# Low parts of weight chunks by ScalarE and an accumulating DMA, selection steps at another rate, and value products one portion later

## The chip, the core and the metric

The kernel runs on one core of a Trainium2 chip. The core has a matrix engine (PE, with weight loads shown apart as PEld), three engines for elementwise work (DVE is VectorE, ACT is ScalarE, POOL is GpSimd), an engine that issues DMAs (SP), and 16 DMA engines that all queues share. The metric is the device time of one execution in microseconds (us). One execution of the kernel was profiled; its trace gives every instruction with its start, its duration and what released it.

## What is computed

Two layers of a transformer block over 528 tokens (16 meta tokens ahead of 512) with 1024 channels. Per layer, cut to what matters here:

```python
proj = einsum('btd,de->bte', rms_norm(x), w_in)       # 1024 x 4808 weights
q, k, v, gate_a, u_b, gate_b, q_idx, k_idx, w_idx, merge = split(proj)
q = rope(rms_norm(q)); k = rope(rms_norm(k)); q_idx = rope(q_idx); k_idx = rope(k_idx)
score = sum_h relu(q_idx . k_idx) * w_idx             # 8 index heads
sel   = top_k(score, 128)                             # of the visible keys, per query
attn  = softmax(q . k over sel) @ v                   # 8 heads of 64
y_a   = (attn * silu(gate_a)) @ w_a
y_b   = (pool(u_b) * silu(gate_b)) @ w_b
out   = x + (sig(merge_a) * y_a + sig(merge_b) * y_b) @ w_out
```

Nothing is rounded to fewer bits on the way to the output: a product of float32 matrices is made of three products of a faster format (F32R), high x high, high x low and low x high, where the high part is the value rounded to that format and the low part is what is left.

## The kernel before, in words

**Weights.** They come in 54 chunks of 2048 columns per partition, 27 per layer, used in a fixed order: one for keys and values, two for index queries, two for gate_b, two for u_b, one for half of the queries, two for gate_a, one for the other queries, two for w_b, then eight for the merge gates (`mixed` chunks, prepared otherwise), two for w_a and four for w_out. A chunk is two raw halves of 128 x 1024 float32. `w_load` (L128) issues their DMAs on SP; there are three raw buffers, so a half is loaded when an older half is no longer read. For each half, preparation makes a high tile and a low tile of 128 x 1024 F32R, out of eight such tiles (tag `w`): `high` (L174) is a copy by ACT, `low` (L178) is a subtraction, raw minus high, by DVE. The items wait in `prep_q`; while a chunk is in use, the next one is prepared, and each finished group of matmuls takes one item (`group_done`, L295). What is left when the chunk is needed is done at once (`flush_prep`).

**Order.** PE and DVE do their instructions in the order in which the program writes them. ACT, POOL and the DMA queues are ordered by a planner at build time, which may move an instruction ahead of others that were written earlier.

**The selection.** Top-128 is 16 rounds over the score tiles of 128 queries: find the eight largest (MAX8), then overwrite them (MATCH_REPLACE8). Query tiles are taken in pairs, first the tiles 0 and 1, then the tiles 2 and 3 (with 400 and 528 keys); a half-round is one `yield` of `topk_steps` (L604), that is, MAX8 or MATCH_REPLACE8 for both tiles of the pair. The steps wait in `sel` and are slipped in between other DVE work by an account in `group_done`: every call on PE or DVE adds a price from `pe_cost` or `dve_cost` to a meter, and

```python
spare[0] += FULL * (pe.us - seen[0]) - (dve.us - seen[1])
spare[0] = min(spare[0], CAP)                  # CAP = 1.5
while spare[0] > 0 and sel:                    # one half-round, its price taken off
```

A DVE call over n elements per partition has the price 0.15 + 0.00104 n us. ACT, POOL and DMA calls have none. Whatever is left of the selection when its result is needed is done at once: `ensure(2)` (L1094), called by `logits` (L629) for the first head pair of the query tile 2, runs all the half-rounds left of tiles 2 and 3, one after the other.

**Attention.** A generator (L626 to L735) whose portions are pumped between the matmul groups of other work (w_b, then the merge gates). For head pair u of 16 there are three portions: `logits(u+1)`, `scale(u)` and `values(u-1)`; then `soft(u+1)` (DVE adds the selection mask, ACT takes the exponential) and `gated`; then `turn(u)` (PE transposes the probabilities, ACT copies them out of PSUM as `pt`, L684). `values` multiplies `pt` by V on PE (tag `v`).

**Query groups.** `q_post` (L532) handles each group of the two query chunks: two DVE products, ACT squares, DVE sums them, `inv_rms` (L409) adds a small constant (L411) and takes the power -0.5 (L412), both on POOL, and DVE multiplies by the result.

Of the kernel before, what the change touches and what calls it, by code (L numbers as in the profile page):

```python
# [10 lines left out]
AF = mybir.ActivationFunctionType  # L11
OP = mybir.AluOpType
# [9 lines left out]
EPS = 1e-6  # L22
# [5 lines left out]
NCOL = 968  # L28
LB = 6
R_ATT = (1.8, 1.7)  # L30
FULL = 0.88
CAP = 1.5
W0 = 3
LAG0 = 2
# [53 lines left out]
def tile_block(ctx: ExitStack, tc: tile.TileContext, x, meta, w_in, pool_w, w_a, w_b, w_out, rows, hgain, c_tab, out):  # L88
    nc = tc.nc
    act, gp = nc.scalar, nc.gpsimd  # L90
    pe, dve = Metered(nc.tensor, pe_cost), Metered(nc.vector, dve_cost)
# [16 lines left out]
    def w_rows(w, c0, cols):  # L108
        return w.rearrange("(k p) e -> p k e", p=128)[:, :, c0:c0 + cols]

    chunks = []
    mixed = set()
    for l in range(2):
        wi = w_rows(w_in[l], 0, w_in.shape[2])
        chunks.append([(wi[:, :, 512:640], 0), (wi[:, :, 2688:2816], 128)])
        mb = [3784, 4040, 4296, 4552]
        order = [2176, 2432, 1664, 1920, 1408, 1152, 0, 640, 896, 256]
        chunks += [[(wi[:, :, c:c + 256], 0)] for c in order]
        chunks += [[(w_rows(w_b[l], c, 512), 0)] for c in (0, 512)]
        mixed |= set(range(len(chunks), len(chunks) + 8))  # L120
        chunks += [[(wi[:, :, c:c + 256], 0)] for c in (*mb, 2760, 3016, 3272, 3528)]
        chunks += [[(w_rows(w_a[l], c, 512), 0)] for c in (0, 512)]
        chunks += [[(w_rows(w_out[l], c, 256), 0)] for c in (0, 256, 512, 768)]

    W = {"load": 0, "prep": 0, "use": 0}
    raws, ready = {}, {}

    def w_load():  # L128
        c = W["load"]
        if c >= len(chunks):  # L130
            return
        W["load"] += 1
        kt = chunks[c][0][0].shape[1]
        cols = 2048 // kt
        raws[c] = []
        for s in range(2):
            r = wpool.tile([128, kt // 2, cols], F32, tag="raw", name="raw", bufs=3)
            for src, o in chunks[c]:
                nc.sync.dma_start(r[:, :, o:o + src.shape[2]], src[:, s * kt // 2:(s + 1) * kt // 2, :])
            raws[c].append(r)  # L140

    prep_q = deque()
# [8 lines left out]
    def w_tile():  # L151
        return wpool.tile([128, 1024], F32R, tag="w", name="w", bufs=8)

    def w_prep_enqueue(eng=dve):
        c = W["prep"]
        if c >= len(chunks):
            return
        W["prep"] += 1
        kt = chunks[c][0][0].shape[1]
        cols = 2048 // kt  # L160
        ready[c] = {}
        if c in mixed:
            prep_q.extend(mixed_prep(c))
            return
        parts = ready[c] = ([], [])

        def split(which):
            t = w_tile().rearrange("p (k e) -> p k e", e=cols)
            parts[which].extend(t[:, k] for k in range(kt // 2))
            return t  # L170

        his = {}

        def high(s):  # L174
            his[s] = split(0)
            act.copy(his[s], raws[c][s])  # L176

        def low(s):  # L178
            eng.tensor_sub(split(1), raws[c][s], f(his[s]))
            if s == 1:  # L180
                del raws[c]
                w_load()

        def second():
            low(0)
            high(1)

        prep_q.extend((lambda: high(0), second, lambda: low(1)))

    def mixed_prep(c):  # L190

# [103 lines left out]
    def group_done():  # L295
# [9 lines left out]
        half_done()  # L305
        spare[0] += FULL * (pe.us - seen[0]) - (dve.us - seen[1])
        spare[0] = min(spare[0], CAP)
# [58 lines left out]
    mhalf = one.tile([128, 1], F32, name="mhalf")  # L366
# [39 lines left out]
            gp.tensor_tensor(tab, ctab, bc(g), op=OP.mult)  # L406
            gp.tensor_tensor(w.rearrange("p t (a d) -> p t a d", a=2), s4, sw(g), op=OP.mult)

    def inv_rms(o, i):  # L409
        if i is not None:  # L410
            gp.tensor_scalar(o, i, EPS, None, op0=OP.add)  # L411
        gp.tensor_tensor(o, o, mhalf[:o.shape[0], :1].to_broadcast(list(o.shape)), op=OP.pow)  # L412

    hhi = one.tile([128, KT, T], F32R, name="hhi")
    hlo = one.tile([128, KT, T], F32R, name="hlo")
# [116 lines left out]
    def q_post(t, ps, normed, dst):  # L532
        s, m = TOK[t]
        p3 = ps[:m, :256].rearrange("p (h d) -> p h d", h=4)
        t1 = tmp.tile([128, HB], F32, tag="tt", name="t1", bufs=6)
        t2 = tmp.tile([128, HB], F32, tag="tt", name="t2", bufs=6)
        v1 = t1[:m, :256].rearrange("p (h d) -> p h d", h=4)
        C, S = (Cq[:m, t], Sq[:m, t]) if normed else (ctab[:m, t], stab[:m, t])
        dve.tensor_tensor(v1, p3, C[:, None, :].to_broadcast([m, 4, 64]), op=OP.mult)
        dve.tensor_tensor(t2[:m, :256].rearrange("p (h a d) -> p h a d", h=4, a=2), swapped(ps[:m, :256], 4),  # L540
                          S.rearrange("p (a d) -> p a d", a=2)[:, None, :, :].to_broadcast([m, 4, 2, 32]), op=OP.mult)
        if normed:
            sq = tmp.tile([128, HB], F32, tag="tt", name="sq", bufs=6)
            act.activation(sq[:m, :256], ps[:m, :256], AF.Square, scale=HD ** -0.5)  # L544
            ss = small(4, "ss4")
            dve.tensor_reduce(ss[:m], sq[:m, :256].rearrange("p (h d) -> p h d", h=4), axis=AX.X, op=OP.add)
            rq = small(4, "rq")
            inv_rms(rq[:m], ss[:m])
        gp.tensor_tensor(t1[:m, :256], t1[:m, :256], t2[:m, :256], op=OP.add)  # L549
        if normed:  # L550
            qs = tmp.tile([128, 544], F32R, tag="L", name="qs", bufs=LB)[:, :512].rearrange("p (h c) -> p h c", h=4)
        else:
            qs = tmp.tile([128, 4, 128], F32R, tag="P", name="qs", bufs=3)

        def second():
            if normed:
                dve.tensor_tensor(v1, v1, rq[:m, :, None].to_broadcast([m, 4, 64]), op=OP.mult)
            act.copy(qs[:m, :, 0:64], v1)

        def third():  # L560
            dve.tensor_sub(qs[:m, :, 64:128], v1, f(qs[:m, :, 0:64]))

        def trans():
            tp = bank("a", F32R)
            for h in range(4):
                pe.transpose(tp[:, h * 128:h * 128 + m], qs[:m, h, :], identr[:m, :m])
            act.copy(dst, f(tp).rearrange("p (h c) -> p h c", h=4)[:, :, :m])
        later(second, 1)
        later(third, QN if normed else QI)
        later(trans, QN + 1 if normed else QI + 1)  # L570
# [55 lines left out]
    def attention(ensure):  # L626
# [17 lines left out]
        def soft(u):  # L644
            i, j = divmod(u, 4)
            n = NK[i]
            mn, sm = small(2, "mn"), small(2, "sm")
            L = {}
            for hh, pi, o, w, ps in st[u]:
                if pi == 0:  # L650
                    L[hh] = tmp.tile([128, 544], F32, tag="L", name="lt", bufs=LB)
                e = min(w, n - o)
                dve.tensor_tensor_reduce(L[hh][:, o:o + e], ps[:, :e], SC[i][:, n - 1::-1] if i == 0 else SC[i][:, o:o + e], 1.0,
                                         3e38 if pi == 0 else mn[:, hh:hh + 1], op0=OP.add, op1=OP.min,
                                         accum_out=mn[:, hh:hh + 1])
            for hh in range(2):
                act.activation(L[hh][:, :n], L[hh][:, :n], AF.Exp, scale=-1.0, bias=mn[:, hh:hh + 1],  # L657
                               accum_out=sm[:, hh:hh + 1])
            st[u] = L, sm

        def scale(u):
            i, j = divmod(u, 4)
            n = NK[i]
            L, sm = st[u]
            rs = small(2, "rs")
            dve.reciprocal(rs, sm)
            for hh in range(2):
                act.activation(L[hh][:, 16:n], L[hh][:, 16:n], AF.Copy, scale=rs[:, hh:hh + 1])  # L668
                dve.tensor_scalar(pms[i][:, 2 * j + hh, :], L[hh][:, 0:16], rs[:, hh:hh + 1], None, op0=OP.mult)
            st[u] = L  # L670
# [45 lines left out]
        for u in range(-1, 17):  # L716
            if u + 1 < 16:
                logits(u + 1)
            if 0 <= u < 16:
                scale(u)  # L720
            if u >= 1:
                values(u - 1)
                if u % 4 == 0:
                    meta_values(u // 4 - 1)
            yield
            if u + 1 < 16:
                soft(u + 1)
            if u >= 1 and u % 4 == 0:
                gated(u // 4 - 1)
            yield  # L730
            if 0 <= u < 16:
                turn(u)
                if u % 4 == 3:
                    meta_turn(u // 4)
            yield  # L735
# [217 lines left out]
    for l in range(2):  # L953
# [98 lines left out]
        for c in (1, 0):  # L1052
            w = chunk()
            for mi in (1, 0):
                j = 2 * c + mi
                u = tmp.tile([128, 544], F32, tag="L", name="u", bufs=LB)
# [158 lines left out]
        else:  # L1215
            for c in range(4):
                w = chunk()
                for t in range(1, 5):
                    s, m = TOK[t]
                    hf = 0 if t <= 2 else 1  # L1220
                    o = s - hf * HB
# [66 lines left out]
```

## Time and profile before

| | |
|---|---|
| median of 3 runs | 850.3 us (850.09, 850.3, 850.82) |
| the profiled execution | 851.3 us |
| its span, first to last instruction | 849.5 us |
| mean granted TensorE clock | 0.96 of full speed |
| instructions | 15773 |

The profiled execution is 1.8 us longer than its span: that lies ahead of the first and behind the last instruction. It is 1.0 us above the median. A row of the groups gives the operation, its tiles (written <- read), the count, the busy time in all and the mean of one in ns, then the idle time before it and what ended that. A row of the waits gives who waited for whom, the sum in us, how often, and the longest. In the table of stretches, each engine has its busy time and, in brackets, its instructions; PEclk is the granted clock.

### The profile page before, as it was taken

Reading aid. Unit: us, or ns where it says so; the run is one execution under the profiler, and the core shown is the slowest. Engines: PE = TensorE matmul, PEld = TensorE weight load, DVE = VectorE, ACT = ScalarE, POOL = GpSimd, SP = SyncE. Lnnn points to the kernel's source line nnn. Section 1 sums busy time; section 2 is a strip of 40 time slices with the busy share of each in tenths; the row PEclk is TensorE's granted clock in tenths of the full one; section 3 lists DMA queues with packets and bytes.
Section 4 is the critical chain, followed back from the end, with each engine's and each line's share of the span. In section 5 each row is a group of like instructions: output and inputs, shape, how many; then the busy total and the mean of one; then the engine's idle time right before and its main releaser. Section 6 shows DMA issues by size and latency. Waiting matters only on the chain.

```text
span 849.5 us, 15773 instructions
## 1 busy us (share of the span) xinstructions
PE 768.4 (90%) x5989; PEld 727.4 (86%) x5989; DVE 623.9 (73%) x1452; ACT 438.7 (52%) x1016; POOL 242.5 (29%) x266
## 2 busy tenths in 40 slices
PE   7999999987980999999999999999889269999998
PEld 5999999987870888999999989989768269999998
DVE  6776887759889776576447768878799987766622
ACT  5556534236760778643344565252568148874421
POOL 6540165063310121124345301642532011212400
PEclk9999999988995899999999999999999769999999
DMA  8422222211120121252513222221203003117231
GB/s 268 154 77 73 76 75 64 100 51 51 50 75 0 51 75 51 77 200 91 185 54 99 77 73 77 74 78 72 75 26 100 25 25 101 50 51 226 96 110 44
DMA packets 64171, 71.71 MB, mean 84 GB/s; under 512 B 2736, under 2 KB 55248, under 8 KB 64096
## 3 DMA queue, kind: packets, MB, share of 16 engines
q1 hardware_dynamic: 64096, 70.71, 26.5%
q8 instruction: 47, 0.77, 0.4%
q14 instruction: 28, 0.23, 0.1%
HBM read 64.28 MB, written 6.42 MB: 83 GB/s over the span
## 4 chain that ended last, share of the span: by engine, by line
PE 70%; DVE 21%; ACT 4%; POOL 3%; issue 2%; DMA 0%; SPq 0%; ACTq 0%; DVEq 0%; POOLq 0%
PE d L60 57%; PE a L60 10%; DVE sc L60 4%; PE v L60 4%; DVE m L60 3%; DVE w L60 3%; DVE t L60 3%; DVE x L60 1%; DVE hlo L60 1%; POOL rq L412 1%; DVE hsum L60 1%; POOL rq L411 1%; DVE raw L60 1%; DVE pm L60 1%; ACT lt L657 1%
## 5 line engine op out<-in xcount | busy, mean ns | idle before, releaser
L60 PE MATMUL d<-hhi,w 128*128 128x256 f32 (+3 forms) x1408 | 291.3, 298 | 0.0
L60 PEld LDWEIGHTS d<-hhi,w 128*128 128x128 f32 x1408 | 227.9, 190 | 7.3 <-issue 1.4
L60 DVE TENSOR_TENSOR w<-raw,w 128x512 fp32r<-128x512 f32 (+1 forms) x186 | 177.9, 966 | 23.9 <-ACT w L200 14.0
L60 PE MATMUL d<-hlo,w 128*128 128x256 f32 (+3 forms) x704 | 194.4, 295 | 0.6 <-POOL hlo L1155 0.6
L60 PE MATMUL d<-w,hhi 128*128 128x256 f32 (+2 forms) x928 | 145.6, 286 | 3.7 <-ACT w L176 2.7
L60 PEld LDWEIGHTS d<-hlo,w 128*128 128x128 f32 x704 | 133.5, 190 | 3.3 <-POOL hlo L1155 0.8
L60 PEld LDWEIGHTS d<-w,hhi 128*128 128x128 f32 (+1 forms) x928 | 125.7, 186 | 7.8 <-ACT w L176 3.1
L206 POOL TENSOR_TENSOR raw<-raw 128x512 f32<-128x512 f32 x32 | 41.6, 1302 | 237.3 <-DVE w L60 157.2
L176 ACT CAST w<-raw 128x1024 fp32r<-128x1024 f32 x76 | 79.5, 1049 | 16.8 <-PE d L60 13.9
L200 ACT CAST w<-raw 128x512 fp32r<-128x512 f32 x112 | 67.7, 619 | 34.9 <-POOL raw L206 16.4
L60 PE MATMUL d<-w,hlo 128*128 128x256 f32 (+2 forms) x464 | 85.4, 282 | 0.0
L60 PE MATMUL d<-hsum,w 128*128 128x264 f32 (+1 forms) x576 | 77.4, 289 | 0.0
L60 PEld LDWEIGHTS d<-hsum,w 128*128 128x128 f32 x576 | 72.3, 191 | 1.6 <-issue 1.2
L60 PE MATMUL a<-consts,lt 128*128 128x128 f32 x161 | 25.2, 284 | 51.2 <-ACT lt L668 48.3
L60 PEld LDWEIGHTS d<-w,hlo 128*128 128x128 f32 (+1 forms) x464 | 68.1, 187 | 0.4
L60 PEld LDWEIGHTS a<-consts,lt 128*128 128x128 f32 x161 | 18.9, 143 | 54.0 <-ACT lt L668 50.3
L668 ACT ACTIVATE lt<-lt,rs 128x128 f32<-128x128 f32 (+3 forms) x64 | 32.8, 559 | 53.6 <-DVE rs L60 53.5
L549 POOL TENSOR_TENSOR t<-t,t 128x256 f32<-128x256 f32 (+1 forms) x34 | 32.2, 947 | 95.5 <-DVE t L60 89.2
L60 PE MATMUL d<-mhi,w 128*128 128x272 f32 (+2 forms) x192 | 54.3, 363 | 3.2 <-ACT sq L544 2.9
L60 DVE MATCH_REPLACE8 sc<-m,sc 128x400 f32<-128x400 f32 (+2 forms) x100 | 54.3, 547 | 0.0
L60 DVE MAX8 m<-sc 128x8 f32<-128x400 f32 (+2 forms) x100 | 52.5, 554 | 0.6
L1155 POOL TENSOR_TENSOR hlo<-ta,hhi 128x256 fp32r<-128x256 f32 (+1 forms) x32 | 31.2, 988 | 57.5 <-PE d L60 42.5
(189 smaller groups left out, 1323.5 us busy)
## 6 DMA issues: line engine op xcount, KB each, us to landing
raw<-in_w_in_dram SPq DMA_DIRECT2D x72, 512.0 KB, 3.5
raw<-in_w_out_dram SPq DMA_DIRECT2D x16, 512.0 KB, 3.4
kept<-res SPq DMA_DIRECT2D x16, 264.0 KB, 2.7
res<-kept SPq DMA_DIRECT2D x16, 264.0 KB, 4.9
raw<-in_w_branch_b_dram SPq DMA_DIRECT2D x8, 512.0 KB, 3.6
raw<-in_w_branch_a_dram SPq DMA_DIRECT2D x8, 512.0 KB, 4.4
xt<-in_x_dram SPq DMA_DIRECT2D x4, 512.0 KB, 5.3
raw<-in_w_in_dram SPq DMA_DIRECT2D x8, 256.0 KB, 4.8
```

The source lines that it names most:

```text
L60: return fn(*a, **k)
L176: act.copy(his[s], raws[c][s])
L200: act.copy(t[:, 0], blk[src[n]])
L206: eng.tensor_tensor(blk[src[n]], blk[src[x]], blk[src[y]], op=op)
L411: gp.tensor_scalar(o, i, EPS, None, op0=OP.add)
L412: gp.tensor_tensor(o, o, mhalf[:o.shape[0], :1].to_broadcast(list(o.shape)), op=OP.pow)
L549: gp.tensor_tensor(t1[:m, :256], t1[:m, :256], t2[:m, :256], op=OP.add)
L657: act.activation(L[hh][:, :n], L[hh][:, :n], AF.Exp, scale=-1.0, bias=mn[:, hh:hh + 1], accum_out=sm[:, hh:hh + 1])
L668: act.activation(L[hh][:, 16:n], L[hh][:, 16:n], AF.Copy, scale=rs[:, hh:hh + 1])
L1155: gp.tensor_sub(hlo[:, j, a:a + n], d, f(hhi[:, j, a:a + n]))
```

## The change

Four edits:

1. For ten chunks per layer (gate_b, u_b, queries, gate_a, w_b; the set `by_dma`) the low tile is made in another way: ACT writes minus the rounded raw half (`minus`), and a DMA issued on POOL adds the raw half to it in place. The high tile is a copy by ACT as before (`plus`), but comes after both low tiles. A chunk has four items in `prep_q` instead of three. DVE has no part in these chunks.
2. `FULL`, the share of PE's price that the account of the selection gives to DVE, goes from 0.88 to 1.0.
3. In `attention`, `values(u-1)` and `meta_values` move one portion later, behind `soft(u+1)`, and `gated` moves one portion later too, in front of `turn(u)`. There are three portions per head pair as before.
4. In `q_post`, the addition of the small constant in `inv_rms` moves from POOL to DVE. The power stays on POOL.

```diff
-FULL = 0.88
+FULL = 1.0
...
-    mixed = set()
+    mixed, by_dma = set(), set()
...
         chunks += [[(w_rows(w_b[l], c, 512), 0)] for c in (0, 512)]
+        by_dma |= set(range(len(chunks) - 10, len(chunks)))
...
-        prep_q.extend((lambda: high(0), second, lambda: low(1)))
+        def minus(s):
+            t = split(1)
+            act.activation(t, raws[c][s], AF.Copy, scale=-1.0)
+            gp.dma_start(t, raws[c][s], accum_op=OP.add)
+
+        def plus(s):
+            t = split(0)
+            act.copy(t, raws[c][s])
+            if s == 1:
+                del raws[c]
+                w_load()
+
+        if c in by_dma:
+            prep_q.extend((lambda: minus(0), lambda: minus(1), lambda: plus(0), lambda: plus(1)))
+        else:
+            prep_q.extend((lambda: high(0), second, lambda: low(1)))
...
-    def inv_rms(o, i):
+    def inv_rms(o, i, eng=gp):
+        half = mhalf[:o.shape[0], :1].to_broadcast(list(o.shape))
         if i is not None:
-            gp.tensor_scalar(o, i, EPS, None, op0=OP.add)
-        gp.tensor_tensor(o, o, mhalf[:o.shape[0], :1].to_broadcast(list(o.shape)), op=OP.pow)
+            eng.tensor_scalar(o, i, EPS, None, op0=OP.add)
+        gp.tensor_tensor(o, o, half, op=OP.pow)
...
-            inv_rms(rq[:m], ss[:m])
+            inv_rms(rq[:m], ss[:m], dve)
...
                 scale(u)
+            yield
+            if u + 1 < 16:
+                soft(u + 1)
             if u >= 1:
                 values(u - 1)
                 if u % 4 == 0:
                     meta_values(u // 4 - 1)
             yield
-            if u + 1 < 16:
-                soft(u + 1)
             if u >= 1 and u % 4 == 0:
                 gated(u // 4 - 1)
-            yield
             if 0 <= u < 16:
                 turn(u)
```

## The prediction

> **What bounds the kernel now.** I read the page's first part and its chain, then the waits, then the timeline around the longest wait, then the stretches.
>
> ```profile
> span 849.5 us, 15773 instructions
> PE 768.4 (90%) x5989; PEld 727.4 (86%) x5989; DVE 623.9 (73%) x1452; ACT 438.7 (52%) x1016; POOL 242.5 (29%) x266
> PE 70%; DVE 21%; ACT 4%; POOL 3%; issue 2%; DMA 0%; SPq 0%; ACTq 0%; DVEq 0%; POOLq 0%
> ```
>
> PE carries 70% of the chain that ended last, and DVE 21% although it is idle a quarter of the time: in a few places DVE alone is waited for. The waits, over all the span, say where:
>
> ```profile
> PE a L60 <- ACT lt L668: 48.3, 2, 25.3
> ACT lt L668 <- DVE rs L60: 53.5, 10, 24.1
> DVE t L60 <- POOL rq L412: 13.6, 15, 3.0
> PE v L60 <- ACT pt L684: 7.4, 7, 2.3
> ```
>
> Two waits of PE hold 48.3 us: PE waits for ACT's scaling of the probabilities, and ACT in turn for a DVE reciprocal. The timeline around the first, then around the second:
>
> ```profile
> 250.44 1.17 DVE L60 MAX8 m<-sc 128x8 f32<-128x400 f32 x2
> ...
> 273.51 1.18 DVE L60 MAX8 m<-sc 128x8 f32<-128x400 f32 x2
> ...
> 275.82 0.70 DVE L60 TENSOR_SCALAR sc<-sc 128x400 f32<-128x400 f32 x2
> ...
> 277.18 1.30 PE L60 MATMUL a<-consts,lt 128*128 128x128 f32 x4 [25.35 <-ACT lt L668]
> ```
>
> ```profile
> 661.77 0.56 DVE L60 MATCH_REPLACE8 sc<-m,sc 128x400 f32<-128x400 f32 x1
> ...
> 686.00 0.70 DVE L60 TENSOR_SCALAR sc<-sc 128x400 f32<-128x400 f32 x2
> ...
> 687.43 1.30 PE L60 MATMUL a<-consts,lt 128*128 128x128 f32 x4 [22.95 <-ACT lt L668]
> ```
>
> That is `ensure(2)`: the selection steps left over for query tiles 2 and 3, done in a block while PE stands still. The reader should see the spacing: the timeline has a MAX8 pair every 2.31 us, eleven of them from 250.44 to 273.51 (ten intervals, 23.07 us). So a half-round takes 1.154 us; the first block has 22 half-rounds and the closing TENSOR_SCALAR, the second begins with a MATCH_REPLACE8 and has (686.00 - 661.77) / 1.154 = 21 and the closing.
>
> ```profile
> 60.00:190.00 130.00, 127.11 (x1023) 124.69 (x1022) 97.23 (x217) 56.92 (x118) 46.61 (x54) 0.98 0.25 75
> 190.00:220.00 30.00, 24.13 (x171) 22.37 (x171) 28.33 (x70) 19.83 (x61) 11.28 (x8) 0.86 0.12 36
> 250.00:277.00 27.00, 1.84 (x16) 1.63 (x14) 26.96 (x73) 1.61 (x3) 0.00 (x0) 0.62 0.06 20
> 480.00:606.00 126.00, 123.01 (x797) 110.06 (x797) 98.46 (x208) 56.73 (x108) 41.72 (x47) 1.00 0.25 76
> 606.00:661.00 55.00, 50.04 (x325) 42.88 (x325) 51.79 (x125) 41.15 (x112) 16.25 (x12) 0.95 0.19 58
> 661.00:687.00 26.00, 3.48 (x32) 3.10 (x28) 25.96 (x71) 1.17 (x3) 0.00 (x0) 0.67 0.07 20
> ```
>
> Columns are PE, PEld, DVE, ACT, POOL busy. Three kinds of stretch: 60 to 190 and 480 to 606 (the chunks of this change) are PE's, DVE busy 75 and 78%, ACT 44 and 45%; 190 to 220 and 606 to 661 are DVE's (94%); then the two blocks.
>
> **The selection moves (edits 1 and 2).** I carried the account of `group_done` through, group by group, with the program's own prices. With the constants of before it leaves 23 and 22 items for the blocks, the closing one included, as the trace has them. A low subtraction has the price 0.15 + 1024 x 0.00104 = 1.215 us; from the first queued selection step to the block eight chunks, so 16 of them, fall away: 19.4 us. PE's prices in that stretch sum to 140 us, and 0.12 of that is 16.8 us. A half-round of tiles 2 and 3 is priced at 1.265 us, the 22 at 28 us. Not all of the new allowance is spent, since the account is overdrawn where DVE is overloaded. Carried through with both edits (and 0.15 us for each addition of edit 4) it leaves 4 items in layer 0 and 5 in layer 1, that is 3 and 4 half-rounds and the closing. With FULL alone it would leave 14 and 15, with the subtractions alone 12 and 12. So 19 + 17 = 36 half-rounds leave the blocks: 36 x 1.154 = 41.5 us less standing PE, as the block is DVE from end to end.
>
> What hides them now? In the PE stretches DVE had 22 to 25% idle, and it loses subtractions there:
>
> ```profile
> L60 DVE TENSOR_TENSOR w<-raw,w 128x1024 fp32r<-128x1024 f32 x74 | 96.6, 1311 | 9.4 <-ACT w L176 5.7 <-PE d L60 3.8
> L176 ACT CAST w<-raw 128x1024 fp32r<-128x1024 f32 x76 | 79.5, 1049 | 16.8 <-PE d L60 13.9 <-DMA raw<-in_w_in_dram 2.4 <-ACT w L176 0.3
> ```
>
> Of the 40 (52.4 us) 36 lie in the PE stretches: 36 x 1.311 = 47.2 us go and some 39 us of selection come, so DVE there is no fuller than before. If PE's cover were gone, the steps would cost what they cost in the block.
>
> **Subtractions in DVE's own stretches.** The other four lie where DVE is the bound:
>
> ```profile
> 191.82 2.36 DVE L60 TENSOR_TENSOR w<-raw,w 128x1024 fp32r<-128x1024 f32 x1
> 201.42 1.21 DVE L60 TENSOR_TENSOR w<-raw,w 128x1024 fp32r<-128x1024 f32 x1
> 606.17 1.22 DVE L60 TENSOR_TENSOR w<-raw,w 128x1024 fp32r<-128x1024 f32 x1
> 612.75 2.31 DVE L60 TENSOR_TENSOR w<-raw,w 128x1024 fp32r<-128x1024 f32 x1
> ```
>
> That is 7.1 us; the account puts one more half-round into each of these stretches (2.3 us): 4.8 us gained. Bounds: 0 (PE limits there as soon as DVE is relieved) and 7.1.
>
> **ACT.** 40 more passes of 1024 columns, by the row of the copy 40 x 1.049 = 42 us, nearly all in stretches where ACT is busy under half. On the path only where a copy out of PSUM queues behind them: between 0 and one pass in two (21 us); PE has three result banks, so I take the low side, 2 us.
>
> **POOL and the DMAs.** 40 DMAs are issued on POOL, which waits there for ACT's `minus`; behind it stand the additions and powers of `q_post` and the pooling sums. No row shows an accumulating DMA or one issued by POOL. The nearest are:
>
> ```profile
> raw<-in_w_in_dram SPq DMA_DIRECT2D x72, 512.0 KB, 3.5
> res<-kept SPq DMA_DIRECT2D x16, 264.0 KB, 4.9
> ```
>
> From issue to landing, 3.5 us for the same 512 KB; at the rate of the second row 4.9 x 512 / 264 = 9.5 us. How long may it take? Two first passes of neighbouring chunks:
>
> ```profile
> 137.29 1.05 ACT L176 CAST w<-raw 128x1024 fp32r<-128x1024 f32 x1 [1.41 <-PE d L60]
> ...
> 150.10 1.05 ACT L176 CAST w<-raw 128x1024 fp32r<-128x1024 f32 x1 [0.43 <-PE d L60]
> ```
>
> 12.8 us from chunk to chunk; the first pass ends 1.05 us in, and the low tiles are wanted after two thirds of the next chunk's first group (16 of 24 matmuls at 127.11 / 1023 = 0.124 us, 2.0 us in). So the two DMAs have 12.8 + 2.0 - 1.05 = 13.7 us. At 3.5 us each, even one after the other, they need 7; at 9.5 they are 5.3 us late. I take the same-size row, so no wait of PE, and 1 us for POOL's delays. The raw halves come free later than now (a subtraction less, a landing more), hidden by the same 12.8 us; SP's queue stands behind those releases as it does now. The Trainium skill, page "Collectives: The Full Stack", section "The bandwidth ceiling: the fold count and why AG ≠ RS ≠ AR", says that an add in a DMA engine needs two source reads and so halves the rate; its page "DMA: Bandwidth & Descriptors", section "Anatomy of one DMA — SWDGE (gpsimd) path", gives 2.0 us plus bytes at 436 GB/s for a DMA from GpSimd. An estimate from these two pages is 2.0 + 2 x 1.2 = 4.4 us, with which the sum stays; no run here shows it yet.
>
> **Values later (edit 3).** PE waits 7.4 us in all for `pt`; the portion moved is one stretch of 12 matmuls (1.5 us) longer to wait in. But the waits lie in DVE's stretches, for example
>
> ```profile
> 204.39 0.69 PE L60 MATMUL v<-pt,V 128*64 128x128 f32 x4 [0.77 <-ACT pt L684]
> ...
> 621.45 0.44 PE L60 MATMUL v<-pt,V 128*64 128x128 f32 x4 [2.34 <-ACT pt L684]
> ```
>
> where PE would next wait for DVE. Gain between 0 and 7.4; I take 1.5. `gated` is as far from the next `values` as before.
>
> **The constant on DVE (edit 4).** 18 small DVE instructions (the nearest row is below) against 18 of POOL in a chain DVE, POOL, POOL, DVE:
>
> ```profile
> 276.43 0.15 DVE L60 RECIPROCAL rs<-sm 128x2 f32<-128x2 f32 x1
> L411 POOL TENSOR_SCALAR rq<-ss x18: 216/534/1137, 126.7 to 601.4; 128x4 f32<-128x4 f32 x16, 16x4 f32<-16x4 f32 x2
> ```
>
> DVE gives 18 x 0.15 = 2.7 us and gets back up to 18 x 0.534 = 9.6 us of the 13.6 us it waits for `rq`, all under PE's cover: 0, between 2.7 lost and 2.9 gained.
>
> **The clock.** Behind a standing PE the clock is low for a while:
>
> ```profile
> 202.91 0.70 PE L60 MATMUL a<-KK,qq 128*128 128x144 f32 x2 [2.97 <-DVE mn L60]
> ...
> 203.00:210.00 7.00, 6.23 (x33) 5.70 (x34) 6.15 (x26) 5.85 (x21) 0.00 (x0) 0.59 0.26 78
> 277.00:282.00 5.00, 4.82 (x27) 4.34 (x29) 4.15 (x14) 3.81 (x12) 0.00 (x0) 0.65 0.20 55
> 687.00:695.00 8.00, 7.57 (x41) 7.04 (x41) 6.29 (x17) 5.82 (x16) 2.56 (x2) 0.59 0.23 68
> ```
>
> After the blocks that costs 5 x 0.35 + 8 x 0.41 = 5.0 us. What remains standing is 25.35 - 19 x 1.154 = 3.4 us and 22.95 - 17 x 1.154 = 3.3 us, and a gap of 2.97 us was enough for 0.59. So I count no gain. The Trainium skill, page "TensorE: Matmul & The Clock Gate", section "Part 1: The HAM clock gate (the "warmup" mystery)", has the clock halve after an idle window of about 3.4 us; taken strictly, the two remaining gaps would keep full speed and the sum would be 5.0 us lower, but the row with 2.97 us speaks against taking it strictly.
>
> **Sum**, against the profiled execution of 851.3 us (1.0 above the median): -41.5 - 4.8 + 2 + 1 - 1.5 + 0 = -44.8, so 806.5 there and 805.5 as a median.
>
> **Rivals.** *The accumulating DMA is late (slower).* At 9.5 us each, every by-DMA chunk waits 5.3 us: 20 x 5.3 = 106 on top of 805.5, 912 us. It decides from 44.8 / 20 = 2.2 us of lateness on, that is (13.7 + 2.2) / 2 = 8.0 us per DMA. For it: the only bound is a row of another kind, and the raw buffers hang on the landing too. Against it: the same-size row lands in 3.5, and the DMA engines are busy a quarter of the time.
>
> *The steps move but are not hidden.* The account knows prices, not waits; in the four query chunks DVE goes through the chain with POOL, and the account puts 15.7 more half-rounds there for 8 subtractions less: 15.7 x 1.154 - 8 x 1.22 = 8.3 us if DVE limits; with ACT's upper bound of 21 us, 805.5 + 8.3 + 21 = 835, and some 822 in the middle.
>
> *Nothing moves,* because something else fills DVE before the blocks: 850. The 22 to 25% idle speak against it.
>
> *More than forecast.* The `pt` waits go whole (5.9 more), the clock stays up (5.0), nothing is lost on ACT and POOL (3), the `rq` chain helps (2.9): 789.
>
> **Chances.** Forecast (790 to 818) 0.63; not hidden 0.17; DMA late 0.15; nothing 0.02; more 0.03. Faster 0.83, same 0.02, slower 0.15 (0.2% is about what a measurement of this kernel can tell). The range runs from 789 to 838, which leaves out the late DMA and little else.
>
> **What would show it.** MAX8 pairs in the blocks: one or two instead of eleven. PE's wait for the scaled probabilities: 7 us instead of 48.3. PE waiting for `w` from a DMA: nothing, unless the first rival holds. DVE near 623.9 - 52.4 + 2.7 = 574 us busy, ACT near 438.7 + 42 = 481. If the blocks are short and the time is still over 818, look for PE waits in 60 to 190 and 480 to 606 that were not there.

## The result, and the profile after

The changed kernel takes 809.8 us (median of 3 runs, 809.35 to 810.86) against 850.3: a ratio of 0.9525 [0.9503, 0.9547], 40.5 us less. The forecast was 805.5, with a range from 789 to 838. The profiled execution is the one of 809.35 us, with a span of 807.5, so 42.0 us shorter than the span before.

The page of the changed kernel, its totals and its chain by engine:

```profile
span 807.5 us, 15880 instructions
...
PE 766.4 (95%) x5989; PEld 727.5 (90%) x5989; DVE 578.8 (72%) x1430; ACT 474.6 (59%) x1056; POOL 258.8 (32%) x288
...
PE 75%; DVE 17%; ACT 4%; issue 2%; POOL 1%; DMA 0%; SPq 0%; DVEq 0%; ACTq 0%; POOLq 0%
```

PE has as many matmuls as before and is busy 95% of a shorter span. DVE lost 45 us of work and ACT gained 36. PE's waits in the changed kernel (who waited for whom, sum in us, times, longest):

```profile
PE a L60 <- ACT lt L685: 8.9, 4, 4.5
PE v L60 <- ACT pt L701: 4.6, 3, 4.1
PE a L60 <- DVE mn L60: 3.3, 1, 3.3
```

The wait for the scaled probabilities has gone from 48.3 to 8.9 us. No row of the waits has PE waiting for `w` from a DMA. The timeline of the two blocks, first layer 0, then layer 1:

```profile
253.68 1.17 DVE L60 MAX8 m<-sc 128x8 f32<-128x400 f32 x2
...
255.99 0.70 DVE L60 TENSOR_SCALAR sc<-sc 128x400 f32<-128x400 f32 x2
...
257.36 0.94 PE L60 MATMUL a<-consts,lt 128*128 128x128 f32 x4 [3.54 <-ACT lt L685]
```

```profile
639.35 1.18 DVE L60 MAX8 m<-sc 128x8 f32<-128x400 f32 x2
...
641.66 1.18 DVE L60 MAX8 m<-sc 128x8 f32<-128x400 f32 x2
...
643.96 0.70 DVE L60 TENSOR_SCALAR sc<-sc 128x400 f32<-128x400 f32 x2
...
645.40 1.30 PE L60 MATMUL a<-consts,lt 128*128 128x128 f32 x4 [4.51 <-ACT lt L685]
```

One MAX8 pair is left in layer 0, where eleven stood, and two in layer 1, where ten stood. PE stands 3.54 + 4.51 = 8.05 us there, against 48.3: 40.25 us less. The stretches (PE, PEld, DVE, ACT, POOL busy, then PEclk, DMA share and GB/s):

```profile
60.00:190.00 130.00, 126.89 (x1033) 124.66 (x1032) 98.43 (x255) 74.59 (x138) 52.41 (x63) 0.99 0.66 154
...
480.00:606.00 126.00, 120.98 (x750) 105.16 (x748) 102.69 (x271) 71.97 (x140) 55.36 (x60) 1.00 0.58 134
...
203.00:210.00 7.00, 7.00 (x45) 6.42 (x46) 6.15 (x24) 5.02 (x19) 0.00 (x0) 0.76 0.01 2
257.00:262.00 5.00, 4.57 (x22) 4.37 (x23) 4.50 (x16) 4.10 (x13) 0.00 (x0) 0.67 0.16 40
645.00:653.00 8.00, 7.60 (x40) 7.39 (x41) 6.30 (x17) 5.89 (x16) 2.56 (x2) 0.61 0.23 68
```

From 60 to 190 us PE is as busy as before (126.9 of 130) and DVE too (98.4 against 97.2): the selection steps have taken the place of the subtractions. ACT has 18 us more there. The clock behind the two short gaps is as low as it was behind the long ones (0.67 and 0.61, against 0.65 and 0.59). The row from 203 us lies behind a wait of PE for DVE that both kernels have (3.3 us here, 2.97 before; the clock 0.76 and 0.59).

The DMA issues on the page of the changed kernel:

```profile
w<-raw POOLq DMA_DIRECT2D x40, 512.0 KB, 5.4
```

**Where the 42.0 us come from.** The starts of the same matmuls in both traces, in us from the span's start, cut the span in stretches; each row is the stretch that ends at its matmul, its difference taken from unrounded starts. The last column is PE's idle time in the stretch, before and after:

| matmul | before | after | this stretch | PE idle |
|---|---|---|---|---|
| first `d<-mhi,w`, layer 0 | 178.5 | 179.3 | +0.8 | 7.5, 8.2 |
| first `d<-hsum,w`, layer 0 | 227.8 | 226.1 | -2.5 | 8.8, 8.6 |
| last `a<-KK,qq`, layer 0 | 331.2 | 309.5 | -20.1 | 27.6, 4.9 |
| first `d<-mhi,w`, layer 1 | 595.2 | 572.5 | -0.9 | 3.8, 3.1 |
| first `d<-hsum,w`, layer 1 | 638.4 | 612.3 | -3.3 | 6.2, 5.7 |
| last `a<-KK,qq`, layer 1 | 742.3 | 699.7 | -16.6 | 24.1, 6.6 |
| end | 849.5 | 807.5 | +0.6 | 3.3, 4.0 |

In all, PE is idle 40.0 us less (81.1 before, 41.1 after) and busy 2.0 us less for the same matmuls. The 40.25 us of the two blocks are thus all of the idle time that went; what PE waits elsewhere comes out even. The two stretches with the blocks became only 36.7 us shorter and DVE's own stretches (`mhi` to `hsum`) 5.8, but part of that split depends on where the cut lies. The rows of these four stretches, before and then after:

```profile
178.50:227.80 49.30, 40.54 (x289) 38.17 (x287) 40.40 (x98) 28.69 (x84) 20.03 (x19) 0.86 0.11 33
227.80:331.20 103.40, 75.83 (x624) 70.56 (x623) 84.29 (x230) 61.12 (x150) 13.04 (x10) 0.88 0.19 57
595.20:638.40 43.20, 37.05 (x193) 29.75 (x191) 37.76 (x91) 26.74 (x73) 18.60 (x16) 0.92 0.15 49
638.40:742.30 103.90, 79.79 (x660) 75.17 (x659) 89.71 (x236) 64.58 (x157) 15.64 (x12) 0.89 0.21 62
```

```profile
179.30:226.10 46.80, 38.23 (x276) 36.04 (x275) 41.44 (x102) 27.66 (x80) 21.08 (x18) 0.89 0.20 46
226.10:309.50 83.40, 78.50 (x634) 73.83 (x635) 67.11 (x185) 63.02 (x154) 12.97 (x10) 0.96 0.24 71
572.50:612.30 39.80, 34.10 (x180) 27.08 (x179) 37.56 (x103) 27.15 (x73) 19.41 (x16) 0.96 0.23 54
612.30:699.70 87.40, 80.77 (x672) 76.50 (x671) 73.16 (x194) 66.10 (x160) 15.50 (x12) 0.96 0.24 73
```

By edit 3, 12 `values` matmuls per layer now come behind the first `hsum` product instead of ahead of it. DVE's own stretches lost 13 matmuls each and 5.3 us of busy PE in all, and the block stretches gained 10 and 12 matmuls and 3.7 us. So the 3.5 us by which the block stretches fall short of 40.25 are matmuls that moved over the cut. In the run with edit 3 undone (below) the cut lies as before: there DVE's own stretches are 2.7 us shorter than in the kernel before, and the block stretches 37.6.

DVE has no less work in its own stretches: 79.0 us after, 78.2 before. The instructions on `m`, which are the selection's, take these times there, before and then after (DVE busy, PEclk, DMA share and GB/s):

```profile
178.50:227.80 49.30, 3.80 (x10) 0.86 0.11 33
595.20:638.40 43.20, 3.66 (x8) 0.92 0.15 49
```

```profile
179.30:226.10 46.80, 9.68 (x24) 0.89 0.20 46
572.50:612.30 39.80, 10.96 (x26) 0.96 0.23 54
```

13.2 us of selection came in, about eleven half-rounds, for 11.5 us of subtractions on `w` that went. What became less there is DVE's idle time.

### The profile page after: what moved, and what is told of

Read it like the earlier page. It is cut to its first block, busy times and chain, and to the rows that moved or that the text cites. A ratio compares the mean times of both kernels' runs of the same rounds, so it can differ in the third digit from the quotient of the medians.

```text
span 807.5 us, 15880 instructions
## 1 busy us (share of the span) xinstructions
PE 766.4 (95%) x5989; PEld 727.5 (90%) x5989; DVE 578.8 (72%) x1430; ACT 474.6 (59%) x1056; POOL 258.8 (32%) x288
## 3 DMA queue, kind: packets, MB, share of 16 engines
q1 hardware_dynamic: 64096, 70.71, 27.6%
## 4 chain that ended last, share of the span: by engine, by line
PE 75%; DVE 17%; ACT 4%; issue 2%; POOL 1%; DMA 0%; SPq 0%; DVEq 0%; ACTq 0%; POOLq 0%
PE d L60 61%; PE a L60 10%; PE v L60 4%; DVE t L60 3%; DVE sc L60 2%; DVE w L60 2%; DVE m L60 2%; DVE x L60 2%; DVE hsum L60 1%; DVE hlo L60 1%; DVE raw L60 1%; DVE pm L60 1%; DVE lt L60 1%; DVE ta L60 0%; ACT lt L674 0%
## 5 line engine op out<-in xcount | busy, mean ns | idle before, releaser
L60 PE MATMUL d<-hhi,w 128*128 128x256 f32 (+3 forms) x1408 | 294.3, 299 | 0.2 <-ACT zb L1134 0.2
L60 DVE TENSOR_TENSOR w<-raw,w 128x512 fp32r<-128x512 f32 (+1 forms) x146 | 125.8, 873 | 21.2 <-ACT w L216 11.9
L60 PE MATMUL d<-hsum,w 128*128 128x264 f32 (+1 forms) x576 | 79.8, 291 | 4.8 <-DVE w L60 2.8
L192 POOL DMA_DIRECT2D w<-raw x40 | 36.7, 930 | 102.5 <-ACT w L191 82.5
L60 PE MATMUL d<-mhi,w 128*128 128x272 f32 (+2 forms) x192 | 51.7, 346 | 3.1 <-ACT sq L561 3.1
L191 ACT ACTIVATE w<-raw 128x1024 fp32r<-128x1024 f32 x40 | 41.6, 1057 | 11.2 <-PE d L60 9.5
L60 DVE SCALAR_TENSOR_TENSOR sc<-r,wsg,sc 128x144 f32<-128x144 f32 (+3 forms) x56 | 32.4, 582 | 21.8 <-ACT r L601 19.7
L566 POOL TENSOR_TENSOR t<-t,t 128x256 f32<-128x256 f32 (+1 forms) x34 | 29.7, 872 | 46.4 <-DVE t L60 45.2
L177 ACT CAST w<-raw 128x1024 fp32r<-128x1024 f32 x36 | 37.6, 1048 | 10.8 <-PE d L60 8.0
```

The costliest lines, as they stand in the source:

```text
L60: return fn(*a, **k)
L191: act.activation(t, raws[c][s], AF.Copy, scale=-1.0)
L192: gp.dma_start(t, raws[c][s], accum_op=OP.add)
```

## The experiments

Differences between kernels that ran on different chips are taken from their ratios to the kernel before, times 850.3 us.

**Edit 1 alone** (`FULL` stays 0.88, `values` and the constant as before):

```diff
+        by_dma |= set(range(len(chunks) - 10, len(chunks)))
...
+        if c in by_dma:
+            prep_q.extend((lambda: minus(0), lambda: minus(1), lambda: plus(0), lambda: plus(1)))
```

> The kernel before with edit 1 alone (ACT and the accumulating DMA make the low parts; FULL stays 0.88, values and the constant as before). Theory (the gain is the selection that leaves the two blocks): the account leaves 11 and 12 items instead of 23 and 22, so 12 + 10 half-rounds leave, 22 x 1.154 = 25.4 us, and 2 to 5 us more where DVE was the bound: 820 to 823 us. Rival (the DMA way costs ACT and POOL time that is on the path): 830 or more. Rival (steps move but are not hidden): 835 or more.

823.5 us, ratio 0.9686 [0.9668, 0.9705]: 27 us less, at the upper end of what was expected.

```profile
PE a L60 <- ACT lt L685: 23.6, 3, 11.5
```

Blocks of about half the length are left, as the account says.

**Edit 2 alone:**

```diff
-FULL = 0.88
+FULL = 1.0
```

> The kernel before with FULL 1.0 alone; DVE keeps all its subtractions. Theory: the account leaves 13 and 14 items, so 10 + 8 half-rounds leave the blocks, 20.8 us, hidden in DVE's idle quarter: 829 to 832 us. Rival (without the relief of DVE the steps are not hidden): 840 to 850 us. Rival (the DMA edit is what brings nearly all): 845 or more.

834.7 us, ratio 0.9807 [0.9794, 0.9820]: 16 us less, and 2 to 5 us short of what was expected.

```profile
PE a L60 <- ACT lt L668: 28.2, 3, 13.7
```

Without the relief of edit 1 the steps are hidden less well: the standing PE fell by 20.1 us and the time by 16, and PE's other idle time grew by 5.7 us. With edit 1 alone the other idle time fell by 1.0 us. The two edits alone make 43 us together, all four 40.5, so the two gains nearly add up; a kernel with these two edits and no other was not run.

**Edit 3 undone in the changed kernel** (`values` one portion earlier again):

```diff
-            yield
-            if u + 1 < 16:
-                soft(u + 1)
             if u >= 1:
                 values(u - 1)
...
             yield
+            if u + 1 < 16:
+                soft(u + 1)
...
+            yield
             if 0 <= u < 16:
```

> The changed kernel with values and gated where they were before (edit 3 undone). Theory (the waits for pt lie where DVE is the bound, so moving them matters little): 809 to 812 us. Rival (the later portion saves PE's waits for pt whole): 815 to 817 us, with the PE waits for pt back at 7 us or more.

810.7 us, ratio 0.9531 [0.9516, 0.9546], no measurable difference from the changed kernel.

```profile
PE v L60 <- ACT pt L701: 7.4, 6, 2.3
```

The `pt` waits are back at 7.4 us (4.6 in the changed kernel) and the time is the same. The changed kernel has waits of PE instead that this run does not have, 2.8 us for `w` from DVE and 1.9 for `p` from ACT, while this run waits 2.0 us more for `mn` and 1.9 for `c`, both from DVE.

**Edit 4 undone in the changed kernel:**

```diff
-            inv_rms(rq[:m], ss[:m], dve)
+            inv_rms(rq[:m], ss[:m])
```

> The changed kernel with the small constant added on POOL again (edit 4 undone). The account leaves one item fewer in each block (2 x 1.154 = 2.3 us less standing PE), the chain of the query groups is longer by up to 0.5 us per group. Theory (that chain is under PE's cover): 807 to 810 us. Rival (the chain limits the query groups): 812 to 816 us.

807.5 us (804.8 to 811.5), ratio 0.9488 [0.9463, 0.9512]: some 3 us faster than the changed kernel by the medians, with intervals that just overlap. DVE waits 13.0 us for `rq` again instead of 7.0, at no cost that the time shows, while the blocks are shorter. In the timeline PE stands before them:

```profile
256.37 1.30 PE L60 MATMUL a<-consts,lt 128*128 128x128 f32 x4 [2.31 <-ACT lt L685]
```

```profile
644.50 0.95 PE L60 MATMUL a<-consts,lt 128*128 128x128 f32 x4 [3.28 <-ACT lt L685]
```

That is 2.31 + 3.28 against 3.54 + 4.51 us: a half-round less per block, because the additions no longer use up DVE's allowance in the account.

**The cost of edit 1 without its relief**, in the kernel before: an extra ACT pass and an extra DMA on POOL for each half of the ten chunks. DVE keeps its subtractions.

```diff
         def high(s):
             his[s] = split(0)
             act.copy(his[s], raws[c][s])
+            if c in by_dma:
+                act.copy(his[s], raws[c][s])
+                spill = dram.tile([128, kt // 2, cols], F32, name=f"spill{c}_{s}")
+                gp.dma_start(spill, raws[c][s])
```

> The kernel before with the cost of edit 1 and none of its relief: for each half of the ten chunks a second ACT copy and a plain DMA of the raw half to DRAM issued on POOL; DVE keeps all subtractions and the account is as before. The extra copies and DMAs are extra work only. Theory (ACT and POOL have room, as in the sum: 2 + 1 us): between 0 and 10 us slower than before, most likely 3; the waits of PE for the scaled probabilities stay at 48 us. Rival (the load of ACT, POOL and the DMA engines sits on the path and eats a good part of the gain): 20 us slower or more, with new PE waits for ACT between 60 and 190 us.

870.5 us, ratio 1.0238 [1.0222, 1.0255]: 20 us slower, as the rival had it. But the loss has two places. By the starts of the matmuls the kernel is 9.1 us behind at the first index scores of layer 0, and it loses 8.6 more between the last `a<-KK,qq` of layer 0 and the first index scores of layer 1; all the rest adds 1.2 us. The timeline at the first place:

```profile
31.33 0.79 POOL L181 DMA_DIRECT2D spill<-raw  x1 [8.35 <-DMA raw<-in_w_in_dram]
...
34.51 0.23 DVE L60 TENSOR_TENSOR t<-d,Sk 128x64 f32<-128x64 f32 x1 [6.37 <-POOL t L514]
...
35.88 1.32 PE L60 MATMUL d<-w,hhi 128*128 128x200 f32 x3 [3.36 <-ACT hhi L435]
```

The planner had put the issue of the DMA on POOL ahead of small additions and powers. The DMA reads the raw half, which was still on its way from DRAM, so POOL stood 8.35 us, behind it DVE, ACT, and in the end PE, and then the clock was low (0.50 from 35.8 to 47 us). That is not how the changed kernel's DMA stands: it waits for `minus`.

**The same, with the DMA reading what ACT has just made:**

```diff
-                gp.dma_start(spill, raws[c][s])
+                gp.dma_start(spill, f(his[s]))
```

> As the run with the cost of edit 1 alone, but the extra DMA writes out the high tile that ACT has just made instead of the raw half, so that its issue on POOL waits for ACT's pass, as the accumulating DMA does, and not for the raw half to arrive from DRAM. Extra work only. In the run before this one POOL stood before such an issue for 103.4 us waiting for raw from DRAM, and at 32 and 469 us PE lost 9 us each time behind the additions and powers that were queued there. Theory (the 20 us were that order on POOL, not the load of ACT or of the DMA engines): 0 to 6 us slower than the kernel before, and the PE gaps for hhi at 32 and 469 us are gone. Rival (the load itself costs): 15 us slower or more again.

854.1 us, ratio 1.0044 [1.0029, 1.0059]: 3.7 us slower, between 2.5 and 5.0. PE's waits for `hhi` in this kernel:

```profile
PE d L60 <- ACT hhi L435: 0.7, 2, 0.4
```

In the run above, that row had 7.0 us. At the first index scores of both layers this kernel is only 0.5 and 0.6 us behind. So 40 ACT passes and 40 plain DMAs of 512 KB cost about the 3 us of the sum, and the 16 us more were that order on POOL: POOL waited 124 us for raw halves there and 0.8 here. That a DMA which reads the raw half also holds its buffer is not the cause, since ACT waits 2.7 us for raw halves in both.

**One and three further DMAs of the raw half ahead of each accumulating one**, in the changed kernel (shown with one; three have `range(3)`):

```diff
         def minus(s):
             t = split(1)
             act.activation(t, raws[c][s], AF.Copy, scale=-1.0)
+            for i in range(1):
+                spill = dram.tile([128, kt // 2, cols], F32, name=f"spill{c}_{s}_{i}")
+                gp.dma_start(spill, raws[c][s])
             gp.dma_start(t, raws[c][s], accum_op=OP.add)
```

> The changed kernel with one more DMA of the same raw half (512 KB, to DRAM) issued on POOL ahead of each accumulating DMA, so four DMAs per chunk instead of two; extra work only. By the trace of the changed kernel one of them keeps the 16 DMA engines busy for 2.9 us, so a pair becomes 4 x 2.9 = 11.6 us and a lead of some 2.5 us: just about the 13.7 us that the prediction gave the pair. Theory (lateness costs only beyond that budget): 0 to 8 us slower than the changed kernel. Rival (the landing is on the path already): 40 us slower or more (2.9 us or so for each of 20 chunks, twice).

> As the run with one more DMA, with three more ahead of each accumulating one: eight per chunk, 8 x 2.9 = 23 us of the DMA engines where the chunk has 13.7 us. Theory (beyond the budget the lateness goes to PE one for one): 23 + 2.5 - 13.7 = 12 us late per chunk, 20 chunks, so 190 to 240 us slower than the changed kernel, with PE waiting for w from a DMA; at the least 100 us. Rival (raw buffers or the order of the planner take it up): under 40 us slower.

866.6 us, ratio 1.0184 [1.0170, 1.0198], so 56 us slower than the changed kernel; and 902.8 us, ratio 1.0616 [1.0602, 1.0631], so 93 us slower. Neither the theory's figure nor the rival's fits both, and neither run says much on the landing: these DMAs read the raw half, so POOL stops at them as above (with one of them, 8.46 us at 31.57 us in the trace), and PE waits above all for `qs` and `us`, which come through POOL (16.7 and 6.0 us), not for `w` from a DMA (in the second 9.2 us, 3 times). The expectations also took 2.9 us of the DMA engines for a plain DMA; the last section has what it is.

**A later landing, without a stop for raw:** the extra DMA reads the low tile, so it comes after `minus`, and the accumulating DMA has to wait until it has read. First with one, then with two (`range(2)`):

```diff
             act.activation(t, raws[c][s], AF.Copy, scale=-1.0)
+            for i in range(1):
+                spill = dram.tile([128, kt // 2, cols], F32, name=f"spill{c}_{s}_{i}")
+                gp.dma_start(spill, f(t))
             gp.dma_start(t, raws[c][s], accum_op=OP.add)
```

> The changed kernel with one DMA of the low tile to DRAM issued ahead of the accumulating DMA, which has to wait until the first has read the tile: from minus to the landing it is then about 3.2 + 5.4 = 8.6 us or more instead of 5.4, near the 8.0 us of the prediction's late DMA. Extra work only. Theory (a pair of DMAs has 13.7 us, and the two halves overlap in part): the second tile lands 9 to 14 us after the first minus, so 0 to 10 us slower than the changed kernel. Rival (the landing is on PE's path already): 3.2 us or more for each of the 20 chunks, 60 us slower or more, with PE waiting for w from a DMA.

829.2 us, ratio 0.9749 [0.9717, 0.9782]: 19 us slower than the changed kernel, more than the theory's 0 to 10 and far from the 60 of the rival. By the medians of its page the extra DMA lands after 3.1 us and the accumulating one 5.3 us after its own issue, so some 8.4 us in all. PE does not wait for `w` from a DMA at all. ACT waits instead. All the waits, the rows with raw, in this kernel:

```profile
ACT w L191 <- DMA raw<-in_w_in_dram: 20.8, 8, 5.3
...
ACT w L191 <- DMA raw<-in_w_branch_b_dram: 11.7, 2, 7.8
```

In the changed kernel these waits are 1.6 us (2 times, 1.0 the longest). One place in the timeline shows what follows:

```profile
68.47 1.06 ACT L191 ACTIVATE w<-raw 128x1024 fp32r<-128x1024 f32 x1 [5.34 <-DMA raw<-in_w_in_dram]
69.43 0.57 ACT L587 CAST qi<-a 128x512 fp32r<-128x512 f32 x1
...
70.05 0.53 PE L60 MATMUL a<-identr,qs 128*128 128x128 f32 x4 [2.14 <-ACT qi L587]
```

A late landing holds a raw buffer longer, the next raw half is loaded later, ACT stands in `minus` for it, and the copies out of PSUM behind `minus` reach PE late.

> As the run with one DMA of the low tile ahead of each accumulating one, with two: the DMA engines then have 6 x 2.9 = 17.4 us of work per chunk on this way, and the second tile lands about 20 us after the first minus. Extra work only. Theory (what lies over 13.7 us goes to PE): 4 to 8 us late per chunk, 20 chunks, so 80 to 160 us slower than the changed kernel, with PE waiting for w from a DMA in the chunks of the edit. Rival (the order of the items gives more room than the 13.7 us): under 40 us slower.

862.7 us, ratio 1.0145 [1.0122, 1.0167]: 53 us slower than the changed kernel, between the theory and its rival. ACT waits 56.7 us for raw halves (38.9 + 17.8), and now PE waits for the tile as well:

```profile
PE d L60 <- DMA w<-raw: 20.4, 8, 5.8
```

**One extra DMA, with four raw buffers instead of three** (the tags L and B have one tile less each, to make room):

```diff
-            r = wpool.tile([128, kt // 2, cols], F32, tag="raw", name="raw", bufs=3)
+            r = wpool.tile([128, kt // 2, cols], F32, tag="raw", name="raw", bufs=4)
```

> The run with one DMA of the low tile ahead of each accumulating one, with four raw buffers instead of three; to make room, the tags L and B have one tile less each (5 and 8), which may cost something in the attention. In the run with three raw buffers, ACT's minus waited 32.5 us (10 times) for a raw half from DRAM, and PE's waits for qi, qs and sila stood behind that; PE did not wait for w once. Theory (the late landing holds a raw buffer, the next load starts late, and ACT stands in minus with copies for PE behind it): with a fourth buffer ACT's waits for raw fall below 10 us, the first merge product of layer 0 comes at 180 to 183 us instead of 189, and the whole at 812 to 820 us instead of 829. Rival (POOL's queue, or the landing itself, delays PE): 826 to 833 us, and the first merge product near 189 us.

813.4 us, ratio 0.9567 [0.9551, 0.9583]: only 4 us behind the changed kernel, 15 us better than with three buffers and the same DMAs. ACT's waits for a DMA in this kernel, all of them:

```profile
ACT junk L943 <- DMA xt<-in_x_dram: 1.6, 2, 1.4
...
ACT junk L943 <- DMA mt<-in_meta_tokens_dram: 0.5, 1, 0.5
...
ACT identr L384 <- DMA consts<-in_tables_dram: 0.4, 1, 0.4
```

None is for a raw half. The first merge product of layer 0 comes at 182.7 us (189.0 with three buffers, 179.3 in the changed kernel). So most of the cost of a late landing goes by the raw buffers, as the theory had it. The extra DMA's landing even holds POOL longer than with three buffers (26.2 us against 12.0), so that wait is not what cost the 15 us. The 4 us left may be the landing, POOL or the smaller tags; no run separates them. Nor was the fourth buffer run without the extra DMA, but in the changed kernel ACT waits only 4.2 us for raw halves (1.6 in `minus`, 2.6 in a copy), so it has little to win there.

**FULL at 1.1, with the constant on POOL**, in the changed kernel:

```diff
-FULL = 1.0
+FULL = 1.1
...
-            inv_rms(rq[:m], ss[:m], dve)
+            inv_rms(rq[:m], ss[:m])
```

> The changed kernel with the small constant added on POOL as before (edit 4 undone) and FULL at 1.1 instead of 1.0. The account then leaves no selection step for either block. Theory (the steps are still hidden beside PE): 3 + 5 half-rounds less than the changed kernel at 1.154 us are 9 us, of which some go back into the stretches ahead: 801 to 806 us. Rival (DVE is full by now, so the steps cost where they go what they cost in the block): 807 to 812 us, with the PE waits for DVE ahead of the blocks grown.

800.4 us (799.1 to 802.4), ratio 0.9417 [0.9405, 0.9430]. This beats both kernels, by 50 and 9 us, and lies just under the time expected. Against the run with the constant on POOL alone the step of `FULL` is worth 6 us, and the intervals are apart. PE's wait for the scaled probabilities, then the stretches where the blocks were:

```profile
PE a L60 <- ACT lt L685: 0.2, 1, 0.2
```

```profile
250.00:255.00 5.00, 4.93 (x42) 4.33 (x41) 4.96 (x17) 3.78 (x11) 0.00 (x0) 1.00 0.21 52
255.00:265.00 10.00, 10.00 (x83) 9.69 (x83) 8.49 (x24) 8.91 (x26) 2.57 (x2) 1.00 0.25 81
...
642.00:650.00 8.00, 8.00 (x70) 7.70 (x69) 7.07 (x20) 6.57 (x17) 0.00 (x0) 1.00 0.05 7
```

No block is left, PE does not stand, and the clock stays at 1.00. The span is 10.2 us shorter than the changed kernel's, of which 8.05 us were PE standing in the blocks. Elsewhere two waits of PE for DVE grew, for `mn` from 3.3 to 5.1 us and for `qs` from 0.7 to 4.2, so the steps are not hidden for nothing. PE is busy 2.8 us less for the same matmuls; the clock that now stays up fits that, which was not tested by itself.

## Why the prediction was right, and where it was off

The mechanism, the sign and the time were right: 806.5 us forecast for the profiled execution, 809.35 found, 2.9 us over. By its steps:

- **Selection, -41.5.** Measured -40.25. The account's three and four half-rounds were three and five, so one of 1.154 us stayed in layer 1. The signs that were named came as named: one or two MAX8 pairs, 8.9 us of PE waiting for the scaled probabilities against 7, DVE at 578.8 us busy against 574, ACT at 474.6 against 481. Edits 1 and 2 alone leave about half of the blocks each, as the account carried through for each of them has it.
- **"Hidden", at no cost.** It held to about 2 us: outside the blocks PE is idle 33.0 us, 32.8 before, and 35 with edit 3 undone. The rival "not hidden" lies 16 to 29 us over the forecast and failed: from 60 to 190 us PE is as busy as before.
- **Subtractions in DVE's own stretches, -4.8.** These stretches are 5.8 us shorter, but only 2.7 where edit 3 does not move matmuls over their end, so the agreement in size is luck. With edit 1 alone they are 4.9 us shorter. The step that failed is the account's one more half-round in each of them, 2.3 us in all: about eleven went there, 13.2 us, and DVE's work there did not fall.
- **ACT +2, POOL and the DMAs +1.** The run with that cost alone lost 3.7 us, from 2.5 to 5.0, with plain DMAs in place of the adding ones.
- **Values later, -1.5.** 0.5 by the medians, which can't be told from nothing. The `pt` waits fell by 2.8 us, but other waits took their place, not all of them for DVE.
- **The constant on DVE, 0.** Undoing it wins about 3 us by the medians (not firmly, the intervals overlap), at the edge of the bounds given. (The upper bound of 2.9 doesn't follow from its own figures, 9.6 - 2.7 = 6.9.) The step that failed is that the additions were priced as DVE time under PE's cover. They also use up the account, and that left a half-round more in each block, where it is not under cover: 2.3 us. The prediction had the additions in the account, so these half-rounds are in its -41.5, but it did not charge them to this edit. The 6 us less of waiting for `rq` bought nothing.
- **The clock, 0.** 0.67 and 0.61 behind the short gaps, so nothing was gained. The Trainium skill, page "TensorE: Matmul & The Clock Gate", section "Part 1: The HAM clock gate (the "warmup" mystery)", sets the drop after an idle window of about 3.4 us. Both gaps left are longer than that, so they do not test it. A wait of PE for `sq` of 3.11 us in the same trace does (behind it the clock was 0.50 from 187.9 to 193.7 us), and so does the run with the constant on POOL: behind its gap of 2.31 us the clock was 0.53 for 3.6 us,

```profile
256.40:260.00 3.60, 3.53 (x16) 3.34 (x17) 2.79 (x9) 2.61 (x8) 0.00 (x0) 0.53 0.00 0
```

so the strict reading, 5.0 us of the sum, is not borne out here.

- **The sum.** The forecast was 2.9 us too low. The blocks gave 1.25 us less than it said and DVE's own stretches, at 2.7 instead of 4.8, 2.1 less; what the smaller terms were worth can't be told from nothing.
- **The accumulating DMA is late.** It lands in 5.4 us, not the 3.5 that was taken and far from the 9.5 of the other end, and no PE wait for `w` arose. The working behind the rival was wrong all the same. "The two DMAs have 13.7 us" looked for the room between `minus` and PE's first use of the tile, and let the raw buffers be "hidden by the same 12.8 us". The rotation of the raw buffers is the tighter limit: in the changed kernel ACT just gets its raw halves (1.6 us of waits), and 3 us more per landing cost 19 us, with no wait of PE for the tile. With a fourth buffer 4 us more per landing (4.1 and 5.4 by the medians) cost 4. By the rule of the prediction 8.4 us per DMA would have been 2 x 8.4 - 13.7 = 3.1 us late in 20 chunks, 62 us. So the price of lateness was too high, its start too late, and it is paid on another engine. The forecast held because 5.4 us still lies within the room that these runs show.

## What to carry to other kernels

Work that one engine does in a block while another stands was worth its whole length here, because it could go where the first engine has idle time. Check with the stretches that the new place is not full, and keep small instructions out of the account that pays for it, since each one there buys back a piece of the block. When a tile is made by a DMA that reads its source late, the first thing that runs out may not be the tile but the buffer of the source; look at who waits for the next load into that buffer, and what is queued behind it. A DMA issued on POOL stopped POOL here until its input was there, for 8.35 us in one place, so let it read what the neighbouring engine has just made, not what is still on its way.

## What the runs showed of the hardware

The adding DMA keeps the 16 DMA engines busy for longer than a plain one of the same bytes. The queue rows, first of the changed kernel (40 adding DMAs), then of the run with 40 plain ones that read ACT's tile:

```profile
q0 software_dynamic: 5760, 20.97, 14.4%
```

```profile
q0 software_dynamic: 5760, 20.97, 6.2%
...
spill<-w POOLq DMA_DIRECT2D x40, 512.0 KB, 3.7
```

0.144 x 807.5 / 40 = 2.9 us each, against 0.062 x 852.2 / 40 = 1.3: 2.2 times, for the same number of packets. The Trainium skill, page "Collectives: The Full Stack", section "The bandwidth ceiling: the fold count and why AG ≠ RS ≠ AR", has the rate of a collective's add halved by its second source read; these two rows agree in size. The plain DMAs go to DRAM and the adding ones stay on the chip, so the rows do not separate the add from the target. With the formula of the Trainium skill, page "DMA: Bandwidth & Descriptors", section "Anatomy of one DMA — SWDGE (gpsimd) path", that had led to the prediction's estimate of 4.4 us for the landing; the 5.4 us measured decide, and the estimate was nearer to them than the row of the same size. In landing time the factor is only 5.4 / 3.7 = 1.5. On POOL the issue of an adding DMA takes 0.93 us and that of a plain one 0.59 (the groups' means of these two kernels).
